# A decoder step with paged attention and a state-space branch: the issue order as a written list instead of a planner in the kernel

## The chip, the cores and the metric

The kernel runs on one core of a Trainium2 chip. The time is the device time of one execution in microseconds (us), here that of the only core. The core has five engines, each with an instruction queue of its own that is worked through in order: PE (matrix products), DVE (vector work), ACT (activations), POOL (a second vector engine, which also issues the gathers from the paged cache) and SP (which only issues transfers). ACT issues some small transfers as well. The trace is of one profiled execution.

## What is computed

One step of a trunk layer for a prompt of 512 tokens and, beside it, one new token for each of 8 running sequences with 4096 cached tokens. Everything is float32.

```python
def _pre(x, c, ...):                      # adaLN, RMSNorm, one input projection
    mod = silu(c) @ w_ada + b_ada
    shift, scale, gate = split(mod, 3)
    h = _rmsnorm(x, g_norm) * (1 + scale) + shift
    q, k, v, z_att, fl, u, z_ssm = split(h @ w_in, ...)
    logf = log_sigmoid(fl + b_fgate)
...
    o_att = _fox_prompt(q, k, v, logf)    # prompt: causal softmax(q k^T/8 + cum_i - cum_j) v
    y_ssm, h_re, h_im = _s5_scan(u, ...)  # complex diagonal recurrence
...
    k_past = cache_k[page_table]          # sample: 8 sequences x 4096 rows x 8 heads x 64
    v_past = cache_v[page_table]
    lf_past = cache_logf[page_table]
    o_att = _fox_sample(q, k, v, logf, k_past, v_past, lf_past)
...
def _post(...):
    att = o_att * silu(z_att)
    g = gelu(y_ssm)
    ssm = g * sigmoid(g @ w_glu + b_glu) * silu(z_ssm)
    return x + gate * (concat(att, ssm) @ w_out)
```

A final RMSNorm follows. The outputs are the two results, the new keys, values and log-forget gates, and the final states. The cached K and V that have to be read are 64 MB each, against some 20 MB of weights.

## The kernel before

The Python program records every engine call instead of issuing it. `Engine.__getattr__` hands each call to `Plan.add`, which makes a **step** of it; calls on PE that run side by side in the array (the four column strips of one product, for example) join the step before. There are 2881 steps, numbered in the order of recording: 1081 on PE, 712 on DVE, 792 on ACT, 235 on POOL, 61 on SP. `Plan.order()` then puts them in an order with a model of the chip: every step has a modelled cost, the steps that it depends on, and a key

```python
op.key = i - BEHIND * behind[i] + (TURN[i // GRP] if i // GRP < len(TURN) else 0)
```

where `i` is the step's number, `behind[i]` the modelled work that follows from it, and `TURN` a number for each group of 20 steps. Whenever an engine of the model comes free, it takes the ready step with the smallest key. On PE a ready step of the same tile shape is preferred if its key is less than `STAY = 150` higher. `issue()` (L427 to L429) emits the calls in that order, and each engine's queue on the chip holds its own steps in that order. All instructions therefore carry the line L429 and are told apart by engine, operation and tiles. Before an instruction an engine waits for whatever its operands need; the order of the queue is never changed on the chip.

The parts that the text speaks of:

- **The start.** SP loads `w_ada` in eight pieces of 1 MB (steps up to 20, L527), the prompt `x` in two halves (16 and 17, L523) and the first pieces of `w_in` (118 to 121). ACT squares the rows of x (86, 87), POOL makes the reciprocal roots (90 and 91, L597/598), ACT scales the four blocks of x by them (92 to 95, L651), PE transposes x (142 and following, L737). Beside that PE multiplies the conditioning vectors with the eight pieces of `w_ada` (96 to 103, L657), ACT copies the result out (104, L660), PE transposes it (105 to 108, L663), and DVE adds the bias (110, L670). DVE meanwhile builds the tables of the state-space branch. Step 527 (L1434) is the load of `d_skip` into the late part of arena A, on ACT's queue.
- **The cache.** Per sequence there are 8 K tiles and 8 V tiles of 128x2048 (1 MB each), 128 gathers in all, issued by POOL (`gather`, L634). A K tile is multiplied by the query, by POOL (128x1024 of it) and DVE (`dec_k`, L1307), and summed by ACT and DVE into the scores `sc`; `dec_soft` makes the softmax of a sequence; `dec_v` (L1345) multiplies a V tile with the weights on PE, eight matmuls of 128x32 into the tile `pv`. The tiles take five slots: three of the ring `kva` (tile `kv`) and two of arena A (`arA`); a gather waits until its slot has been used up.
- **The prompt.** Projections, state-space branch, attention and the output projection (L1594, six to ten pairs of 128x128 matmuls into `mm` at a time) share PE with the V products. Four small loads of `b_ada` (steps 1588 to 1591, L1467) go out on ACT's queue into arena B (`arB`), and the load of `w_glu` (1592, L1486) on SP's.
- **The tail.** After the last V tile come small matmuls for the sample rows (L1353, L1391, L1405), the samples' output projection and norm, and the stores.

The transfers of POOL, and those of SP and ACT, have their completion signals in rotation, eight for each of the two groups: a new issue of the same turn waits until the transfer eight before it has landed. The loads of ACT share the rotation with those of SP.

Of the kernel before, what the change touches and what calls it, by code (L numbers as in the profile page):

```python
# [13 lines left out]
BF16 = mybir.dt.bfloat16  # L14
# [22 lines left out]
TICK = 10240 / 3  # L37
BEHIND = 0.0005
STAY = 150
GRP = 20  # L40
XAT = 5
TURN = [
# [9 lines left out]
]  # L52
# [23 lines left out]
LAT = {"PE": (200, 5), "DVE": (190, 127), "ACT": (165, 200), "Pool": (90, 100), "SP": (90, 0)}  # L76
ACT_SET = {AF.Exp: 0, AF.Silu: 1, AF.Sin: 1, AF.Gelu_apprx_tanh: 2, AF.Sigmoid: 3, AF.Identity: 1}


class Op:  # L80
    __slots__ = ("eng", "calls", "cost", "dma", "deps", "tiles", "func", "tail", "load", "cols", "key", "mode", "lock",
                 "row", "desc")


class Engine:
    def __init__(self, plan, name, eng):
        self._p, self._n, self._e = plan, name, eng

    def __getattr__(self, method):
        return lambda *args, **kw: self._p.add(self._n, method, getattr(self._e, method), args, kw)  # L90


class Ring:


    def __init__(self, plan, pool, bufs, psum=False):
        self.p, self.pool, self.bufs, self.psum = plan, pool, bufs, psum

    def tile(self, shape, dtype, name, bufs=None):
        n = bufs or self.bufs  # L100
        t = self.pool.tile(shape, dtype, name=name, bufs=n)
        self.p.own(t, (id(self), name), n, self.psum)
        return t
# [25 lines left out]
class Plan:  # L129
    def __init__(self):  # L130
        self.ops, self.info, self.hist, self.rings = [], {}, {}, {}

    def own(self, t, ring=None, bufs=1, psum=False):
        a = t[:]
        w = int(np.prod(t.shape[1:]))
        self.info[a.tensor.name] = (w, ring, psum)
        if ring is not None:
            self.rings.setdefault(ring, (bufs, []))[1].append(a.tensor.name)

    def region(self, x):  # L140
        x = getattr(x, "ap", x) if isinstance(x, bass.IndirectOffsetOnAxis) else x
        if isinstance(x, (int, float, str, list, tuple, type(None))) or not hasattr(x, "to_broadcast"):
            return None
        a = x if hasattr(x, "offset") else x[:]
        i = self.info.get(a.tensor.name)
        if i is None:
            return None
        w = i[0]
        ap = [list(d) for d in a.ap]
        m = 1  # L150
        for step, n in ap[:0:-1]:
            if step:
                o = m
                if n > 1 and step > 0:
                    k = 1
                    while k < n:
                        j = min(k, n - k)
                        m |= m << (step * j) if j == k else m << (step * (n - k))
                        k += j
        size = int(np.prod([n for _, n in ap[1:]]))  # L160
        p0 = a.offset // w
        return a.tensor.name, p0, p0 + (ap[0][1] if ap[0][0] else 1), m << (a.offset % w), size, i[2]

    def add(self, eng, method, fn, args, kw):
        out = [args[0] if args else kw["out"], kw.get("accum_out")]
        outs = [r for r in map(self.region, out) if r]
        rest = list(args[1:]) + [v for k, v in kw.items() if k not in ("out", "accum_out")]
        ins = [r for r in map(self.region, rest) if r]
        cost = self.cost(eng, method, args, outs, ins, kw)
        deps, me = set(), len(self.ops)  # L170
        if cost is None:

            me -= 1
            op = self.ops[me]
            op.cost, op.tail = max(op.cost, self.product) + 27, 27
        else:
            op = Op()
            op.eng, op.calls, op.cost, op.deps, op.tiles, op.tail, op.load, op.cols = eng, [], cost, set(), set(), cost, 0, 0
            if eng == "PE":

                x = args[1]
                k, m = x.shape[0], int(np.prod(x.shape[1:]))
                op.load = m / 128 * (27 if x.dtype == BF16 else 107)
                op.mode = tuple(32 if d <= 32 else 64 if d <= 64 else 128 for d in (k, m))
            op.func = ACT_SET.get(args[2]) if method == "activation" else None

            op.lock = "dma" not in method and (eng == "Pool" or eng == "DVE" and (
                sum(not r[5] for r in ins) > 1 or method in ("tensor_copy", "tensor_scalar") and
                not any(r[5] for r in ins + outs)))
            r = (outs or ins)[0]  # L190
            op.dma, op.row, op.desc = self.transfer(args, kw, r) if "dma" in method else (0, 0, 0)
            self.ops.append(op)
        if eng == "PE":
            op.cols += self.columns
        for rw, rs in ((0, ins), (1, outs)):
            for name, p0, p1, m, size, psum in rs:
                h = self.hist.setdefault(name, ([], []))
                for lst in (h[0],) if rw == 0 else h:
                    deps.update(j for j, q0, q1, mm in lst if psum or (q0 < p1 and p0 < q1 and mm & m))
        for name, p0, p1, m, size, psum in outs:  # L200
            h = self.hist[name]
            for lst in h:
                lst[:] = [e for e in lst if not (psum or (p0 <= e[1] and e[2] <= p1 and not e[3] & ~m))]
            h[0].append((me, p0, p1, m))
        for name, p0, p1, m, size, psum in ins:
            self.hist[name][1].append((me, p0, p1, m))
        op.calls.append((fn, args, kw))
        op.deps |= deps - {me}
        op.tiles |= {r[0] for r in outs + ins if self.info[r[0]][1] is not None}

    def transfer(self, args, kw, r):

        total = r[4] * 4 * (r[2] - r[1])
        row = total
        for x in (args[0] if args else kw["out"], args[1] if len(args) > 1 else kw["in_"]):
            if "in_offset" in kw and x is kw["in_"]:
                continue
            a = x if hasattr(x, "offset") else x[:]
            n = 1
            own = a.tensor.name in self.info  # L220
            for step, m in [list(d) for d in a.ap][:0 if own else None:-1]:
                if m > 1 and step != n:
                    break
                n *= m
            row = min(row, n * 4)
        one = 8.5 + row / 25.5
        return max(total / row * one / 16, one), one, total / row / 16

    def cost(self, eng, method, args, outs, ins, kw):
        n = max([r[4] for r in outs + ins], default=1)  # L230
        ps = any(r[5] for r in outs + ins)
        if "dma" in method:
            return (1040 if "indirect" in method else 600) if eng == "Pool" else 480
        if eng == "PE":
            name, lo, hi, _, n, _ = outs[0]
            x = args[2] if method == "matmul" else args[1]
            passes = 2 if method == "transpose" else 1 if x.dtype == BF16 else 4
            self.columns = 0 if lo else n * passes * (ins[0][2] - ins[0][1]) / 128
            row, k = ins[0][1], ins[0][2] - ins[0][1]
            last, self.last_pe = self.last_pe, (name, lo, hi - lo <= 64, row, k <= 64 and method == "matmul")  # L240
# [1442 lines left out]
```

## Time and profile before

| | |
|---|---|
| median of 3 runs | 602.99 us |
| the runs | 595.1, 602.99, 1518.36 us |
| the profiled execution's own time | not listed; its span is 596.7 us |
| instructions | 9245 |
| granted TensorE clock, mean | 0.919 |
| transferred | 176.52 MB, mean 296 GB/s |
| by POOL's queue (q0) | 135.74 MB |
| by the queues of SP and ACT (q1) | 39.40 MB |

In the profile, "idle before" stands in brackets with the engine or transfer that ended it: `[5.51 <-ACT arA L429]` means that the engine stood for 5.51 us until ACT had written `arA`. A `q` behind an engine's name (ACTq) is the issue of a transfer by that engine's sequencer. `x24` behind a row is a number of equal instructions in a row. The chain of waits goes back from the last instruction to whatever released it. The rows of windows give the busy time of each engine in a stretch.

### The profile page before, as it was taken

How to read it: one execution, taken by the hardware profiler on the slowest of the kernel's cores; microseconds unless marked ns; L12 is line 12 of the kernel's file. 1: busy time of each engine (PE TensorE's matmuls, PEld its weight loads, DVE VectorE, ACT ScalarE, POOL GpSimd, SP SyncE). 2: the span in 40 equal slices, each digit the busy share in tenths (PEclk: the TensorE clock that was granted, in tenths of full speed). 3: DMA queues.
4: the chain of work that ended last, by engine and by line, in shares of the span. 5: the costliest groups of instructions: out<-in, count | busy, mean ns of one | idle time of the engine just before them, and what ended most of it. 6: DMA issues, size and time to landing. Idle time of an engine off the chain costs nothing.

```text
span 596.7 us, 9245 instructions
## 1 busy us (share of the span) xinstructions
PE 484.5 (81%) x3158; PEld 227.6 (38%) x3158; DVE 404.3 (68%) x712; ACT 289.2 (48%) x1354; POOL 323.5 (54%) x239
## 2 busy tenths in 40 slices
PE   3543669897888988299989899888589889999884
PEld 2111438743333435076633333333124334333222
DVE  6695899978999885237467957566655644664622
ACT  3043235435057454045463987678728865231301
POOL 6656109537217676255664785586637633864410
PEclk9855899997899999589999989999869989999988
DMA  7993545924409799868999899999979999997961
GB/s 226 391 371 130 163 138 182 362 77 141 142 24 350 267 395 403 344 228 303 393 365 399 302 403 359 359 397 396 389 284 334 356 411 397 370 322 287 372 263 39
DMA packets 45336, 176.52 MB, mean 296 GB/s; under 512 B 6980, under 2 KB 21736, under 8 KB 27880
## 3 DMA queue, kind: packets, MB, share of 16 engines
q0 software_dynamic: 19264, 135.74, 60.1%
q1 hardware_dynamic: 25376, 39.40, 18.8%
q10 hardware_dynamic: 648, 0.78, 0.4%
q8 instruction: 25, 0.41, 0.3%
q14 instruction: 23, 0.19, 0.1%
HBM read 171.48 MB, written 4.42 MB: 295 GB/s over the span
## 4 chain that ended last, share of the span: by engine, by line
PE 31%; DMA 24%; POOL 14%; DVE 13%; ACT 8%; issue 8%; SPq 2%; POOLq 0%; ACTq 0%; DVEq 0%
PE mm L429 22%; POOL kv L429 7%; POOL arA L429 6%; DMA arA<-in_cache_k_dram,kidx 6%; PE pv L429 6%; DMA w<-in_w_glu_dram 4%; DVE sc L429 4%; DVE arA L429 4%; DMA kv<-in_cache_v_dram,kidx 4%; DMA arA<-in_cache_v_dram,kidx 4%; DMA kv<-in_cache_k_dram,kidx 3%; DMA kv<-in_x_prompt_dram 3%; PE tr L429 2%; ACT arB L429 2%; SPq L429 2%
## 5 line engine op out<-in xcount | busy, mean ns | idle before, releaser
L429 PE MATMUL mm<-hT,w 128*128 128x512 f32 x256 | 135.9, 638 | 2.2 <-ACT qk L429 1.1
L429 POOL TENSOR_TENSOR kv<-kv,qs 128x1024 f32<-128x1024 f32 x38 | 90.1, 2373 | 30.9 <-DMA kv<-in_cache_k_dram,kidx 16.2
L429 ACT ACTIVATE kv<-kv 128x64 f32<-128x64 f32 x304 | 73.6, 245 | 55.2 <-DVE kv L429 37.9
L429 DVE TENSOR_REDUCE sc<-kv 128x24 f32<-128x1536 f32 x38 | 66.4, 1746 | 37.3 <-POOL kv L429 37.2
L429 ACT ACTIVATE arA<-arA 128x64 f32<-128x64 f32 (+2 forms) x215 | 52.3, 247 | 58.1 <-DVE arA L429 57.0
L429 POOL TENSOR_TENSOR arA<-arA,qs 128x1024 f32<-128x1024 f32 x26 | 61.8, 2376 | 17.5 <-DMA arA<-in_cache_k_dram,kidx 15.7
L429 POOL DMA_INDIRECT kv<-in_cache_v_dram,kidx x38 | 38.1, 1003 | 44.8 <-PE pv L429 10.8
L429 POOL DMA_INDIRECT kv<-in_cache_k_dram,kidx x38 | 37.4, 983 | 45.4 <-PE tr L429 16.8
L429 DVE TENSOR_REDUCE sc<-arA 128x24 f32<-128x1536 f32 x26 | 45.4, 1746 | 19.0 <-POOL arA L429 18.7
L429 PEld LDWEIGHTS mm<-hT,w 128*128 128x128 f32 x256 | 43.5, 200 | 37.8 <-issue 33.7
L429 ACT ACTIVATION_READ_ACCUMULATOR kv<-kv 128x1 f32 x304 | 57.7, 190 | 0.0
L429 DVE TENSOR_TENSOR kv<-kv,q 128x1024 f32<-128x1024 f32 x38 | 45.9, 1213 | 15.0 <-DMA kv<-in_cache_k_dram,kidx 13.7
L429 POOL DMA_INDIRECT arA<-in_cache_k_dram,kidx x26 | 25.6, 983 | 48.6 <-PE pv L429 24.0
L429 POOL DMA_INDIRECT arA<-in_cache_v_dram,kidx x26 | 25.4, 978 | 46.3 <-ACT arA L429 11.5
L429 PE MATMUL pv<-kv,arA 128*32 128x512 f32 x304 | 42.2, 632 | 9.6 <-DMA kv<-in_cache_v_dram,kidx 7.8
L429 DVE TENSOR_TENSOR arA<-arA,q 128x1024 f32<-128x1024 f32 x26 | 31.5, 1212 | 22.4 <-DMA arA<-in_cache_k_dram,kidx 22.4
L429 DVE TENSOR_TENSOR arA<-arA 128x512 f32<-128x512 f32 (+8 forms) x105 | 39.8, 406 | 1.3 <-ACT arA L429 1.0
L429 ACT ACTIVATION_READ_ACCUMULATOR arA<-arA 128x1 f32 x208 | 39.6, 190 | 0.0
L429 ACT ACT_TABLE_LOAD x26 | 33.4, 1283 | 8.5 <-DVE sc L429 5.0
L429 PE MATMUL pv<-arA 128*32 128x512 f32 x208 | 29.3, 636 | 6.7 <-DMA arA<-in_cache_v_dram,kidx 6.7
L429 PE MATMUL mm<-w,arB 128*128 128x512 f32 x64 | 33.7, 622 | 0.0
L429 PE MATMUL mm<-w,hT 128*128 128x256 f32 x128 | 33.4, 391 | 0.0
(245 smaller groups left out, 866.5 us busy)
## 6 DMA issues: line engine op xcount, KB each, us to landing
w<-in_w_in_dram SPq DMA_DIRECT2D x10, 1024.0 KB
w<-in_w_ada_dram SPq DMA_DIRECT2D x9, 1024.0 KB
qk<-in_w_ada_dram SPq DMA_DIRECT2D x2, 1024.0 KB
kv<-in_x_prompt_dram SPq DMA_DIRECT2D x2, 1024.0 KB
qk<-in_w_in_dram SPq DMA_DIRECT2D x2, 1024.0 KB
w<-in_w_out_dram SPq DMA_DIRECT2D x2, 1024.0 KB
qk<-in_w_out_dram SPq DMA_DIRECT2D x2, 1024.0 KB
hT<-in_x_prompt_dram SPq DMA_DIRECT2D x1, 2048.0 KB
```

The source lines that it names most:

```text
L429: fn(*args, **kw)
```

## The change

`Plan` with its costs, keys, `TURN`, `LAT` and the model is taken out. In its place stands a list `ORDER` of all 2881 step numbers, each once, and a class that issues the recorded steps in it. What `Plan.add` found out about joined PE calls is now said at the call by `join=`. The steps, their engines, their tiles, the rings and the arenas stay as they are.

```diff
-TURN = [
-    -13673, -11809, -11809, -9297, -10336, -3499, 59, -7594, -8009, -2496, -8525, -12911, -12961, -10094,
...
+ORDER = [
...
+]

 class Engine:
-    def __init__(self, plan, name, eng):
-        self._p, self._n, self._e = plan, name, eng
+    def __init__(self, steps, name, eng):
+        self._s, self._e = steps, eng

     def __getattr__(self, method):
-        return lambda *args, **kw: self._p.add(self._n, method, getattr(self._e, method), args, kw)
+        return lambda *args, join=False, **kw: self._s.add(getattr(self._e, method), args, kw, join)
...
+class Steps:
+    def __init__(self):
+        self.ops = []
+    def add(self, fn, args, kw, join):
+        if join:
+            self.ops[-1].append((fn, args, kw))
+        else:
+            self.ops.append([(fn, args, kw)])
+    def issue(self):
+        for i in ORDER:
+            for fn, args, kw in self.ops[i]:
+                fn(*args, **kw)
...
-class Plan:
...
-    def issue(self):
-        for i in self.order():
-            for fn, args, kw in self.ops[i].calls:
-                fn(*args, **kw)
...
-    plan = Plan()
+    plan = Steps()
...
             mm(t[32 * n:32 * n + 32], cs[:, k], wada[k][:, 512 * n:512 * n + 512],
-               start=(k == 0), stop=(k == 7))
+               start=(k == 0), stop=(k == 7), join=n > 0)
```

The list is not the one that `Plan.order()` gives. Compared engine by engine, a step's place differs for 1032 of PE's 1081 steps, 689 of DVE's 712, 753 of ACT's 792, 197 of POOL's 235 and 54 of SP's 61. By the longest common order, 589 steps of PE, 395 of DVE, 533 of ACT, 111 of POOL and 30 of SP have been moved past another one. Places of steps on their engine that the text uses, counted from 0:

| step | engine | what | place before | place in the list |
|---|---|---|---|---|
| 20 | SP | eighth load of `w_ada` | 17 | 13 |
| 96 | PE | first product with `w_ada` | 24 | 48 |
| 101 to 103 | PE | last products with `w_ada` | 63 to 73 | 59 to 61 |
| 142 | PE | first transpose of x | 65 | 86 |
| 90, 91 | POOL | reciprocal roots of x | 28, 29 | 17, 18 |
| 95 | ACT | scaling of the last block of x | 26 | 21 |
| 104 | ACT | copy of the adaLN row | 28 | 22 |
| 110 | DVE | adds the adaLN bias | 155 | 138 |
| 527 | ACT | load of `d_skip` | 11 | 113 |
| 1588, 1589 | ACT | loads of `b_ada` | 263, 272 | 330, 351 |
| 1590, 1591 | ACT | loads of `b_ada` | 273, 275 | 272, 296 |
| 1592 | SP | load of `w_glu` | 35 | 26 |
| 2750 | POOL | last V gather | 230 | 225 |
| 2776 | PE | product of the last V tile | 1065 | 1070 |
| 2838 to 2841 | PE | pairs of the output projection | 1067 to 1073 | 1044 to 1052 |

More of the change, by code (lines that the diff above doesn't have):

```diff
@@ L1 @@
-import heapq
 import math
-from collections import deque
 from contextlib import ExitStack
@@ L36 @@
 BK = 49.375
[L37 to L40, printed above, removed]
 XAT = 5
-TURN = [
[9 rows of a table removed]
-]
 SUF = 5
@@ L70, with __init__ @@
 NEG = -1e30
[L76 to L82, printed above, removed]
+ORDER = [
[151 rows of a table added]
+]
 class Engine:
-    def __init__(self, plan, name, eng):
-        self._p, self._n, self._e = plan, name, eng
+    def __init__(self, steps, name, eng):
+        self._s, self._e = steps, eng
     def __getattr__(self, method):
-        return lambda *args, **kw: self._p.add(self._n, method, getattr(self._e, method), args, kw)
+        return lambda *args, join=False, **kw: self._s.add(getattr(self._e, method), args, kw, join)
 class Ring:
-    def __init__(self, plan, pool, bufs, psum=False):
-        self.p, self.pool, self.bufs, self.psum = plan, pool, bufs, psum
+    def __init__(self, pool, bufs):
+        self.pool, self.bufs = pool, bufs
     def tile(self, shape, dtype, name, bufs=None):
[L100 to L103, printed above, removed]
+        return self.pool.tile(shape, dtype, name=name, bufs=bufs or self.bufs)
+class Steps:
[10 more added lines that the diff above has]
+                fn(*args, **kw)
 class Arena:
@@ L447, in ring @@
     def ring(name, bufs, **k):
-        return Ring(plan, ctx.enter_context(tc.tile_pool(name=name, bufs=bufs, **k)), bufs, "space" in k)
+        return Ring(ctx.enter_context(tc.tile_pool(name=name, bufs=bufs, **k)), bufs)
     cp, sm, wp, qkp, kva = (ring(n, b) for n, b in (("consts", 1), ("small", 2), ("w", 3), ("qk", 2), ("kva", 3)))
@@ L454, in tile_fox_s5_step @@
     arB = ar.tile([128, int(BK * 256)], F32, name="arB")
-    plan.own(arA)
-    plan.own(arB)
     sa = tb = Arena(arA)
@@ L701, in quarters @@
             for j in range(4):
-                mm(t[32 * j:32 * j + 32, 0:w], lhs(k), rhs(k, c0 + w * j, w), start=(k == 0), stop=(k == n - 1))
+                mm(t[32 * j:32 * j + 32, 0:w], lhs(k), rhs(k, c0 + w * j, w), start=(k == 0), stop=(k == n - 1),
+                   join=j > 0)
         return [(slice(c0 + w * j, c0 + w * j + w), t[32 * j:32 * j + 8, 0:w]) for j in range(4)]
@@ L951, in tile_fox_s5_step @@
                     mm(t[32 * j:32 * j + 32, 128 * q + 16 * a:128 * q + 128], Bzf[:, 32 * g + 16 * a:32 * g + 16 * a + 32],
-                       CA[:, g, 0:8 - a], start=(a == 0), stop=(a == 1), skip_group_check=True)
+                       CA[:, g, 0:8 - a], start=(a == 0), stop=(a == 1), skip_group_check=True, join=j > 0)
         ks.append(t.rearrange("p (q x) -> p q x", q=4))
@@ L977, in tile_fox_s5_step @@
         q = k % 4
-        mm(t[32 * q:32 * q + 32], wfl[:, k], hT[:, k], start=(k < 4), stop=(k >= 4))
+        mm(t[32 * q:32 * q + 32], wfl[:, k], hT[:, k], start=(k < 4), stop=(k >= 4), join=q > 0)
     e = sm.tile([128, 512], F32, name="e2")
@@ L1046, in ssm_phase @@
                         mm(t[64 * gh:64 * gh + 64, 256 * i:256 * i + 256], hT[:, k, tau:S:T],
-                           W["u", gh][:, k], start=(k == 0), stop=(k == 7))
+                           W["u", gh][:, k], start=(k == 0), stop=(k == 7), join=gh > 0)
             for i in range(2):
@@ L1085, in ssm_phase @@
                         mm(t[64 * gh:64 * gh + 64, 72 * j:72 * j + 72],
-                           BA[q][:, 4 * gh + j, 64 * i:64 * i + 64], U[:, 4 * q + j, gh])
+                           BA[q][:, 4 * gh + j, 64 * i:64 * i + 64], U[:, 4 * q + j, gh], join=gh > 0)
                 tv.append(t[:, 0:288].rearrange("p (j c) -> p j c", j=4))
@@ L1153, in ssm_phase @@
                     o = t[64 * gh:64 * gh + 64, 128 * j:128 * j + 128]
-                    mm(o, U[:, 4 * q + j, gh, 0:NCH], Toep[:, gh, j, 128 * q:128 * q + 128], start=True, stop=False)
+                    mm(o, U[:, 4 * q + j, gh, 0:NCH], Toep[:, gh, j, 128 * q:128 * q + 128], start=True, stop=False, join=gh > 0)
                     mm(o, Hst[:, g, 0:NCH], CA[:, g, 1:], start=False, stop=True)
@@ L1255, in attn @@
                     r = slice(64 * hh, 64 * hh + 64)
-                    mm(t[hh][:, 0:n], qT[r, m, d], kT[r, m, 0:n], start=False, stop=True)
+                    mm(t[hh][:, 0:n], qT[r, m, d], kT[r, m, 0:n], start=False, stop=True, join=hh > 0)
                 nm = sm.tile([128, 2], F32, name="nm")
@@ L1277, in attn @@
                     mm(o[64 * hh:64 * hh + 64, 128 * kb:], vn[:, kb, 128 * m + 64 * hh:128 * m + 64 * hh + 64],
-                       PT[hh][:, kb, 128 * kb:], start=(kb == 0), stop=(kb == 3), skip_group_check=True)
+                       PT[hh][:, kb, 128 * kb:], start=(kb == 0), stop=(kb == 3), skip_group_check=True, join=hh > 0)
             acopy(attT[:, m], o)
@@ L1345, in dec_v @@
             mm(pv[32 * r:32 * r + 32], pzs[b % 2][:, 4 * c + r], vt[:, 512 * r:512 * r + 512],
-               start=(b % 4 == 0 and c == 0), stop=(b % 4 == 3 and c == 7))
+               start=(b % 4 == 0 and c == 0), stop=(b % 4 == 3 and c == 7), join=r > 0)
         if b % 4 == 3 and c == 7:
@@ L1405, in samp_out @@
                 mm(t[32 * j:32 * j + 32, 0:256], mTs[:, k0 + k],
-                   res["wo"][2 * (j // 2) + k0 // 4][:, k, 256 * (j % 2):256 * (j % 2) + 256], start=(k == 0), stop=(k == 3))
+                   res["wo"][2 * (j // 2) + k0 // 4][:, k, 256 * (j % 2):256 * (j % 2) + 256], start=(k == 0), stop=(k == 3),
+                   join=j > 0)
         o = sm.tile([128, 256], F32, name="e2")
@@ L1480, in gate_part @@
                     mm(gt[32 * j:32 * j + 32, 0:256], cs[:, 2 * i + k], gw[i][:, k, 256 * j:256 * j + 256],
-                       start=(k == 0), stop=(k == 1))
+                       start=(k == 0), stop=(k == 1), join=j > 0)
             V.tensor_add(gsb, gsb, gt[:, 0:256])
```

274 lines of the change are left out of this document (removed), and 159 rows, old and new, of tables (ORDER, TURN).

## The prediction

> **What bounds the kernel now.** I read the page first for the engines and the chain, then windows of 25 us for the stages, then the waits inside those stages.
>
> ```profile
> span 596.7 us, 9245 instructions
> PE 484.5 (81%) x3158; PEld 227.6 (38%) x3158; DVE 404.3 (68%) x712; ACT 289.2 (48%) x1354; POOL 323.5 (54%) x239
> PE 31%; DMA 24%; POOL 14%; DVE 13%; ACT 8%; issue 8%; SPq 2%; POOLq 0%; ACTq 0%; DVEq 0%
> ```
>
> No engine is busy throughout and the chain passes through all of them: the limit changes from stage to stage. The profiled execution's own time is not listed; its span of 596.7 lies 6.3 under the median of 602.99 (the 1518.36 is an outlier) and 1.6 over the run of 595.1. Those two runs differ by 1.3%, so about 2% is what a measurement here tells from no change.
>
> ```profile
> 25.00:50.00 25.00, 7.92 (x35) 2.98 (x35) 20.04 (x41) 8.40 (x15) 14.34 (x2) 0.51 0.94 334
> 75.00:100.00 25.00, 20.26 (x242) 14.89 (x236) 24.35 (x44) 12.77 (x74) 11.42 (x6) 0.93 0.37 128
> 175.00:200.00 25.00, 22.94 (x97) 8.95 (x94) 24.75 (x41) 17.06 (x81) 17.22 (x12) 1.00 0.84 298
> 250.00:275.00 25.00, 21.60 (x149) 15.81 (x149) 11.09 (x17) 10.70 (x69) 12.58 (x9) 0.85 0.65 230
> 375.00:400.00 25.00, 21.36 (x190) 8.93 (x190) 16.10 (x20) 17.00 (x85) 17.03 (x13) 1.00 0.99 377
> 525.00:550.00 25.00, 25.00 (x78) 9.64 (x74) 12.63 (x13) 6.37 (x36) 15.21 (x14) 1.00 0.84 305
> ```
>
> The columns after the window are busy us of PE, weight loads, DVE, ACT and POOL, then granted clock, DMA share and GB/s. Up to about 200 us **DVE** is the limit (24.35 and 24.75 of 25) and the DMA is half empty. From 275 us the **gathers** are (0.99 at 377 GB/s), and from 500 us **PE** shares the limit with them (25.00). The row of 250 to 275 is neither: 230 GB/s, no engine full.
>
> **The change, part by part.** The steps, their engines and their tiles stay; what moves is each engine's queue order. I compared the two orders engine by engine, taking durations from this trace. Nearly every step has another place (1032 of 1081 on PE, 197 of 235 on POOL), but a near one: the mean shift is 11 places on PE, 15 on DVE, 12 on ACT, 2.8 on POOL, 2.7 on SP. So the stages and their limits should stay, and only particular waits change. Building the list happens before the device runs and costs nothing there.
>
> (1) The start. The rows below are of ACT, DVE and POOL.
>
> ```profile
> 28.38 0.28 ACTq L429 DMA_DIRECT2D arA<-in_d_skip_dram  x1
> 28.71 1.19 ACT L429 ACTIVATE arA<-sm 64x512 f32<-64x512 f32 x2 [14.95 <-DMA kv<-in_x_prompt_dram]
> 29.93 0.69 DVE L429 TENSOR_TENSOR arB<-arA 128x512 f32<-128x512 f32 x1 [5.51 <-ACT arA L429]
> 36.56 16.20 POOL L429 TENSOR_SCALAR arA<-arA 128x4 f32<-128x4 f32 x1 [10.66 <-ACT hT L429]
> 52.85 1.05 POOL L429 TENSOR_TENSOR arA<-arA,nhalf 128x4 f32<-128x4 f32 x1
> 61.77 0.37 DVE L429 TENSOR_TENSOR arA<-tr,arA 128x72 f32<-128x72 f32 x2 [9.06 <-PE tr L429]
> 89.35 3.48 DVE L429 TENSOR_TENSOR kv<-kv,q 128x1024 f32<-128x1024 f32 x3 [0.19 <-ACT qs L429]
> 18.36 12.79 SPq L429 DMA_DIRECT2D w<-in_w_ada_dram  x2
> ```
>
> Before 89 us DVE has two large gaps. The first, 5.51 us, waits for ACT copies that stand behind ACT's own issue of the d_skip load (step 527), which was held until a half of x_prompt had landed. The list puts 527 from ACT place 11 to 113, near 100 us of the old clock, so this wait goes. The second, 9.06 us, waits for the transposed adaLN row (step 110). That needs ACT's copy 104, which now stands ahead of three of the four x scalings instead of behind all, and PE's steps 101 to 108, which now stand ahead of the x transposes. But one scaling (step 95) is still ahead of 104, and it needs POOL's steps 90 and 91, the 16.20-us row. That row did not end until DVE stopped. In the list DVE reaches step 110 after about 46 us of work (place 138, before 155), so about half of the gap can stay. Against this, SP's eighth w_ada load (step 20; the second of the 12.79-us row) has been drawn ahead of three other loads and still waits for PE step 96, now behind 36 transposes (place 48, before 24); I estimate a hole in the loads of 3 to 4 us, bounded by nothing and the 12.79 us of that row. Sum: −5.5 −4 to −5 + 4 = about **−5 us**; bounds −14.6 (both gaps gone) and +4. DVE, the limit up to 200 us, carries a lead on to the gathers.
>
> (2) The hole at 250 us.
>
> ```profile
> 243.24 0.79 ACTq L429 DMA_DIRECT2D arB<-in_b_ada_dram  x2
> 244.08 0.60 ACT L429 ACTIVATE arB<-tr 128x512 f32<-128x512 f32 x1 [6.21 <-DMA w<-in_w_in_dram]
> 252.39 0.32 ACTq L429 DMA_DIRECT2D arB<-in_b_ada_dram  x1
> 252.75 0.60 ACT L429 ACTIVATE arB<-tr 128x512 f32<-128x512 f32 x1 [8.07 <-DMA w<-in_w_glu_dram]
> 255.54 0.98 POOL L429 DMA_INDIRECT arA<-in_cache_v_dram,kidx  x1 [11.45 <-ACT arA L429]
> ```
>
> ACT twice stands at the issue of a small b_ada load until a 1-MB SP load has landed, 14.28 us in all; the copies behind it wait, then PE, then POOL's next gather (11.45 us). The window of 250 to 275 moved 230 GB/s where 375 to 400 moved 377: (377−230)·25 us = 3.7 MB, 9.7 us at 377. The list moves two of the four b_ada loads (1588 and 1589) from places 263 and 272 to 330 and 351, 1591 from 275 to 296, leaves 1590 at 272, and puts the w_glu load nine SP places earlier. One at a time they can be held again, where copies stand behind them just the same. Bounds: −9.7, and 0 if the four, held one at a time, stop ACT for as long in all. I take a value near the middle: **−4 us**.
>
> (3) PE's tile shapes.
>
> ```profile
> 412.35 0.86 PE mm L429 x2
> 498.29 2.71 PE pv L429 x24
> 525.34 19.08 PE mm L429 x44
> 546.47 0.99 PE pv L429 x8
> 547.47 1.05 PE mm L429 x2
> 548.52 1.00 PE pv L429 x8
> ```
>
> In the chain, a pair of matmuls of 128x128 among its like takes 0.86 us, and a V product (eight of 128x32) 2.71/3 = 0.90. Where they alternate, the pair takes 1.05 and the product 1.00: 0.29 us for two changes of shape, 0.145 each, or 0.10 if only the product's side is counted. The old order has 353 changes, the list 245; after 475 us 75 and 30. Those 45 cost 4.5 to 6.5 us where PE is full: **−5 us**. The other 63 lie where DVE or the gathers are the limit and count as nothing; without that cover they would be 6 to 9 more.
>
> (4) The tail.
>
> ```profile
> 573.47 0.94 POOL L429 DMA_INDIRECT arA<-in_cache_v_dram,kidx  x1 [1.89 <-PE pv L429]
> 579.06 1.06 PE L429 MATMUL pv<-arA 128*32 128x512 f32 x8
> 584.56 1.10 PE L429 MATMUL mm<-qk,arB 128*128 128x512 f32 x2
> 591.89 0.48 DVE q_s L429
> ```
>
> The last V tile is issued at 573.47 and multiplied at 579.06. Behind it the old order still has 7.8 us of PE work, with output-projection pairs between the small matmuls of the sample rows; the list leaves 3.7, by doing four of those five pairs earlier. 4.1 us at most, nothing if the pairs only push the V product back; PE was full just before, so I take **−1.5 us**.
>
> (5) V tiles held. Five slots take all the gathered tiles, and a gather is issued when its slot is free.
>
> ```profile
> 515.63 0.94 POOL L429 DMA_INDIRECT kv<-in_cache_v_dram,kidx  x1 [0.68 <-DVE e L429]
> 516.60 2.37 POOL L429 TENSOR_TENSOR arA<-arA,qs 128x1024 f32<-128x1024 f32 x1
> kv<-in_cache_v_dram,kidx POOLq DMA_INDIRECT x35, 8.6
> ```
>
> The tile issued at 515.63 lands some 8.6 us later and is used in the product at 546.47, behind the 19.08 us of projection: 22 us lost to one slot of five. Eleven of the 59 V tiles after 195 us wait over 11 us. I summed PE's work ahead of each product in both orders: of eight of them the product comes 6.5 to 13.6 us earlier, together 79 slot-us, 16 us over five slots if each refills at once. Against it POOL's order puts one more multiply (2.37 us) ahead of most V gathers, and four gathers come 10 to 21 us of POOL work later, together 60 slot-us, 12 us. The difference is **−3 us**; bounds −16 and +12, both kept for the range.
>
> Sum: −5 −4 −5 −1.5 −3 = −18.5. From the profiled 596.7 that is 578, from the median 584.5; I state **583**, close to the median because that is the base of the comparison.
>
> **The rivals.**
>
> *Given back* (no change). Parts 1 and 2 bring gathers forward to a time when the DMA is at 0.99, and they queue there; part 5 cancels. Then parts 3 and 4 alone are left: 603 − 6.5 = 596. For it: the DMA share in 375 to 400. Against it: the DMA is at 0.37 and 0.65 in two quoted windows, so bytes do fit earlier.
>
> *POOL's queue turns* (slower). A multiply at the head of POOL waits for its K tile, or for DVE, with a V gather behind it whose slot is free. One multiply of 2.37 us for each of 59 V gathers is 140 slot-us, 28 us over five slots; with the four late gathers 40, less the 16 freed: +24, and +12 if half the multiplies have their K tile ready. With the leads of 1 and 2 lost in the same queue: 615 to 627, say 620. It decides once the added lateness of the V gathers passes the 79 slot-us that PE frees. For it: POOL is in order and has 14% of the chain. Against: K gathers are issued 1 to 10 us of POOL work earlier, so the multiply's tile should be there.
>
> *The start keeps its length.* POOL's two 128x4 rows took 16.20 and 1.05 us; the first ran beside a DVE without a gap, the second as DVE stood. If the second DVE gap only grows by what the first loses, part 1 is nothing: 603 − 13.5 = 589.5. [...]
>
> *All of it pays*: −9 −9.7 −6.5 −4 −8 = −37, 566. It needs the gathers to run at 400 GB/s, while the best quoted window shows 377.
>
> That the list is only the planner's order written down is excluded by the places above.
>
> **The numbers.** Forecast (574 to 592) 0.41; given back 0.21; POOL's queue 0.14; start keeps its length 0.10; all of it 0.14. Faster by over 2% (under 591) is the forecast, all of it, and half of the start case: 0.60. Slower by over 2% (over 615) 0.13, within 2% 0.27. Range **564 to 612**: it takes in every case but the slow one and the far end of the large one.
>
> **What would show it.** Part 1: no 5.51-us gap of DVE near 25 us, and the first K multiply on DVE at 78 to 86 us instead of 89.35. Part 2: the windows from 225 to 300 all over 340 GB/s, ACT's waits behind b_ada below 5 us. Part 3: PE's busy time down by about 10 us in all, from 484.5. Part 4: under 14 us from the last V product to the end (before 17.6). Part 5: the long V waits in the list gone, POOL's idle time before gathers down. I am wrong if POOL or DVE shows new waits for K gathers of over 15 us in all, if the w_ada load holds SP's queue past 30 us, or if the b_ada loads stop ACT again.

## The result and the profile after

The new kernel takes **578.32 us** (median of 4 runs, 576.52 to 581.5) against 602.07 for the old one beside it. The ratio is **0.966, with a 95% interval of 0.958 to 0.974**; in a second comparison it was 0.967 (0.962 to 0.972). The forecast was 583. Ratios here leave disturbed executions out and medians do not, so a ratio can differ a little from the quotient of two medians; three of the traces below (the b_ada loads alone, the eight moved DVE steps, the reverse on the new list) are of disturbed executions, and mainly their local rows are used.

The profiled execution spans 574.5 us, 22.2 less than before. The head, the engines, the chain and the rows of POOL's gathers on the page of the new kernel:

```profile
span 574.5 us, 9192 instructions
PE 471.2 (82%) x3158; PEld 227.6 (40%) x3158; DVE 405.3 (71%) x712; ACT 288.4 (50%) x1353; POOL 315.4 (55%) x239
DMA 35%; DVE 18%; PE 13%; issue 11%; POOL 8%; ACT 5%; POOLq 0%; DVEq 0%; ACTq 0%
L245 POOL DMA_INDIRECT kv<-in_cache_k_dram,kidx x38 | 37.6, 988 | 58.7 <-PE pv L245 13.3
L245 POOL DMA_INDIRECT kv<-in_cache_v_dram,kidx x38 | 37.7, 992 | 42.3 <-PE pv L245 20.2
L245 POOL DMA_INDIRECT arA<-in_cache_k_dram,kidx x26 | 25.2, 969 | 37.4 <-PE pv L245 25.5
L245 POOL DMA_INDIRECT arA<-in_cache_v_dram,kidx x26 | 25.3, 975 | 18.6 <-ACT arA L245 7.6
```

The chain now runs over transfers (35%, before 24%) and much less over PE (13%, before 31%). POOL's idle time ahead of its gathers adds up to 157.0 us. The windows of the new kernel, same columns as before:

```profile
25.00:50.00 25.00, 12.23 (x73) 5.41 (x73) 24.86 (x54) 10.62 (x15) 13.93 (x11) 0.80 0.86 308
175.00:200.00 25.00, 23.77 (x103) 9.14 (x96) 20.31 (x24) 17.46 (x71) 20.27 (x14) 1.00 0.90 325
250.00:275.00 25.00, 23.28 (x181) 15.09 (x174) 13.10 (x19) 12.09 (x65) 15.58 (x11) 1.00 0.97 366
300.00:325.00 25.00, 20.82 (x76) 8.28 (x75) 14.40 (x23) 17.16 (x79) 13.55 (x10) 0.86 0.82 298
525.00:550.00 25.00, 22.69 (x91) 8.16 (x89) 10.57 (x20) 4.26 (x25) 11.06 (x11) 1.00 0.93 368
```

DVE is full from 25 to 50 us (24.86, before 20.04). The hole at 250 is gone (366 GB/s, before 230). But 300 to 325 moves 298 GB/s, where the old kernel moved 386:

```profile
300.00:325.00 25.00, 21.45 (x143) 8.56 (x141) 17.42 (x25) 10.18 (x47) 14.73 (x11) 1.00 1.00 386
```

The clearest view of where the time went compares the same step in two traces. The table gives by how many us a V product starts earlier (minus) than in the old kernel's trace:

| V product (step) | old start | new | start alone | start + b_ada | three edits | rest alone |
|---|---|---|---|---|---|---|
| 1st (1004) | 174.2 | −18.8 | −22.0 | −21.3 | −13.8 | +1.6 |
| 13th (1337) | 262.5 | −23.3 | −11.2 | −23.8 | −25.2 | −3.5 |
| 21st (1612) | 313.2 | −28.2 | −11.1 | −23.1 | −23.6 | −10.8 |
| 25th (1737) | 342.3 | −15.9 | −10.8 | −23.7 | −23.2 | +1.8 |
| 45th (2387) | 477.6 | −12.4 | −11.4 | −22.9 | −23.3 | +4.7 |
| 64th (2776) | 579.1 | −18.3 | −11.3 | −24.3 | −25.9 | +0.2 |
| end | 596.7 | −22.2 | −11.6 | −24.5 | −26.2 | −4.1 |

The column "new" shows that the prediction's sum came out right by parts that were not: 19 us are won before the first V product and 28 by 313 us, 12 are given back by 342 and 3.5 more by 478, then 6 are won up to the last product and 4 behind it. A second trace of the same new kernel has −18.6, −20.9, −26.6, −15.3, −9.6, −13.5 and −17.6 in these rows: the same shape, but up to 5 us apart. A difference of that size between two columns tells nothing by itself. The other columns are the experiments below.

### The profile page after: what moved, and what is told of

It reads as the page before. It is cut to its first block, busy times and chain, and to the rows that moved or that the text cites. A ratio compares the mean times of both kernels' runs of the same rounds, so it can differ in the third digit from the quotient of the medians.

```text
span 574.5 us, 9192 instructions
## 1 busy us (share of the span) xinstructions
PE 471.2 (82%) x3158; PEld 227.6 (40%) x3158; DVE 405.3 (71%) x712; ACT 288.4 (50%) x1353; POOL 315.4 (55%) x239
## 4 chain that ended last, share of the span: by engine, by line
DMA 35%; DVE 18%; PE 13%; issue 11%; POOL 8%; ACT 5%; POOLq 0%; DVEq 0%; ACTq 0%
DMA kv<-in_cache_k_dram,kidx 16%; PE mm L245 9%; DMA kv<-in_cache_v_dram,kidx 7%; DVE arA L245 6%; DMA arA<-in_cache_v_dram,kidx 6%; POOL kv L245 5%; DVE sc L245 5%; DMA arA<-in_cache_k_dram,kidx 4%; PE pv L245 3%; DVE kv L245 3%; POOL arA L245 3%; ACT arB L245 2%; DVE arB L245 2%; ACT kv L245 1%; DVE hT L245 1%
## 5 line engine op out<-in xcount | busy, mean ns | idle before, releaser
L245 PE MATMUL mm<-hT,w 128*128 128x512 f32 x256 | 130.1, 631 | 1.3 <-PE pv L245 0.6
L245 ACT ACTIVATE arA<-arA 128x64 f32<-128x64 f32 (+1 forms) x215 | 52.4, 246 | 50.4 <-DVE arA L245 47.9
L245 POOL DMA_INDIRECT kv<-in_cache_k_dram,kidx x38 | 37.6, 988 | 58.7 <-PE pv L245 13.3
L245 PEld LDWEIGHTS mm<-hT,w 128*128 128x128 f32 x256 | 45.7, 198 | 47.6 <-issue 42.9
L245 DVE TENSOR_TENSOR arA<-arA 128x512 f32<-128x512 f32 (+9 forms) x105 | 45.2, 452 | 0.8
L245 POOL DMA_INDIRECT arA<-in_cache_k_dram,kidx x26 | 25.2, 969 | 37.4 <-PE pv L245 25.5
L245 PE MATMUL mm<-qk,hT 128*64 128x256 f32 x256 | 32.9, 419 | 7.2 <-ACT arA L245 7.0
L245 PE MATMUL pv<-arA 128*32 128x512 f32 x208 | 28.5, 623 | 11.2 <-DMA arA<-in_cache_v_dram,kidx 8.3
L245 POOL DMA_INDIRECT arA<-in_cache_v_dram,kidx x26 | 25.3, 975 | 18.6 <-ACT arA L245 7.6
L245 PEld LDWEIGHTS mm<-qk,hT 128*64 128x64 f32 x256 | 26.1, 201 | 12.9 <-ACT arA L245 7.4
```

What stands on the lines that cost most here:

```text
L245: fn(*args, **kw)
```

## The experiments

### Splitting the list at 180 us

The list is cut at the steps that started before 180 us in the old trace.

```diff
 start alone:  ORDER = [new list's order, steps before 180 us] + [old order, the others]
 rest alone:   ORDER = [old order, steps before 180 us] + [new list's order, the others]
```

> The steps that started before 180 us in the old trace are issued in the new list's order, all later ones in the old order. Theory 'the start carries it': the K and V gathers around 200 us run about 19 us earlier than in the old kernel and the lead is kept, with the hole near 250 us still there: 582 to 588 us. Rival 'given back': the gathers of the middle are bound by the transfers and the lead is used up: 595 to 603 us.

> The reverse: old order up to 180 us, new list's order behind it. Theory 'the start carries it': only the hole (7 us), the giving back (minus 10) and the tail (4 us) are left, so 598 to 603 us. Rival 'the V products and the shapes on PE pay': 588 to 594 us.

Measured: start alone 587.71 us, ratio 0.981 (0.970 to 0.993); rest alone 597.99, ratio **1.000** (0.994 to 1.005). The order of everything behind 180 us, put on the old start, is as a whole worth nothing that can be measured, and the rival (588 to 594 us) falls. That is a sum and not an absence: in its trace a lead of 10.8 us at the 21st product is lost by the 25th, and 9 us are won behind the 45th. But the start alone does not bring the whole gain either: its lead of 22 us at the first V product is 11 at the 13th. Its hole is still there. A piece of its chain (start, us, what), and the ACT row where that piece ends:

```profile
214.05 26.76 DMA w<-in_w_glu_dram
```

```profile
241.20 0.60 ACT L239 ACTIVATE arB<-tr 128x512 f32<-128x512 f32 x1 [9.66 <-DMA w<-in_w_glu_dram]
```

The chain spends 26.76 us on one load of w_glu, because a b_ada issue on ACT stands until that load has landed, and behind it stands a copy that PE's next transposes need (56 matmuls in the chain).

### The hole: the b_ada loads alone, and with the new start

```diff
 ACT's queue, places of 1588, 1589, 1590, 1591:
-263, 272, 273, 275
+345, 346, 347, 348    (behind step 1510, about 300 us)
```

> Old order; only the four b_ada loads stand some 75 to 85 places later on ACT (near 300 us). Theory 'ACT's held issues make the hole at 250 us and it costs the end': no ACT wait behind b_ada, the windows of 240 to 260 us over 340 GB/s, V products at 260 to 300 us 6 to 9 us earlier, and 594 to 597 us. Rival 'given back': the hole is gone but the later gathers are not earlier, 599 to 604 us.

> New list's order up to 180 us, old order behind it, and the four b_ada loads later on ACT as in the kernel with this edit alone. Theory 'start and hole add up': the run with the new start alone gave a ratio of 0.981 and lost 27 us of its chain to the w_glu load behind which b_ada stood; without it 576 to 581 us, all of the new kernel's gain. Rival 'the two leads use the same transfers': 584 to 588 us.

Alone: 595.9 us, ratio **0.990** (0.984 to 0.995). With the new start: 580.49 us, 0.978 (0.967 to 0.990), profiled span 572.1. The window of the hole, alone and then with the new start:

```profile
250.00:275.00 25.00, 22.96 (x124) 15.38 (x125) 16.83 (x24) 11.32 (x69) 16.85 (x13) 0.93 0.96 359
```

```profile
250.00:275.00 25.00, 25.00 (x139) 16.53 (x132) 13.46 (x15) 11.84 (x77) 15.60 (x13) 1.00 0.96 373
```

In both it moves 359 to 373 GB/s, before 230. With the new start the 13th V product is 12.6 us earlier than without the edit (−23.8 against −11.2) and the lead is still there at the end. The two ratios (0.981 and 0.978) have intervals that overlap, so the ratios do not tell the two apart. The times do: all four runs with the edit (573.82 to 583.79 us) lie under all four of the start alone (584.63 to 593.79), though on another chip; the traced run is the fastest of its four. Of the single edit's 10.5 us at the 13th product, 2.3 are left at the end of its trace.

The list itself removes the hole by other means. It issues the w_glu load 37 us earlier, of which its lead at that time explains some 20, and spreads the four b_ada loads:

```profile
226.44 0.40 SPq L429 DMA_DIRECT2D w<-in_w_glu_dram  x1
189.52 0.37 SPq L245 DMA_DIRECT2D w<-in_w_glu_dram  x1
```

In its trace no ACT row from 218 to 285 us waits for a transfer.

### The start: the d_skip load alone

```diff
 ACT's queue, place of 527:
-11
+113
```

> Old order; only the d_skip load (step 527) stands later on ACT, near the place that the list gives it. Theory as predicted: the 5.51-us gap of DVE goes, POOL's row ends 5 us earlier because DVE stops earlier, time 596 to 599 us. Rival 'another wait takes its place': DVE's gap only moves, 601 to 605 us.

595.04 us, ratio **0.991** (0.985 to 0.997). The time lies 1 us under the expected range; the gap and the end of POOL's row came as expected. POOL's row and DVE's remaining gap in its trace:

```profile
33.73 13.40 POOL L239 TENSOR_SCALAR arA<-arA 128x4 f32<-128x4 f32 x1 [7.91 <-ACT hT L239]
56.57 0.37 DVE L239 TENSOR_TENSOR arA<-tr,arA 128x72 f32<-128x72 f32 x2 [9.51 <-PE tr L239]
```

The 5.51-us gap is gone. POOL's row still lasts until DVE stops at 47 us, and the second gap is as long as it was (9.51).

### The start: eight neighbouring DVE steps

In the old order, DVE's last product that reads PSUM (step 281, `arA<-mm,arA`) ends at 36.45 us, just before POOL's row becomes ready at 36.56, and only products with two operands in SBUF follow, for 16 us. Eight neighbours change places; the product that reads PSUM comes 1.2 us later, and three short products (395 to 397, 128x128) come earlier, to just ahead of it:

```diff
 DVE's queue:
-281, 398, 282, 395, 399, 396, 400, 397
+398, 395, 396, 397, 281, 282, 399, 400
```

> Old order; eight neighbouring steps of DVE change places so that one product that reads PSUM (arA<-mm,arA) runs about 1 us later, just when POOL's 128x4 row is ready, inside what was a run of products with both operands in SBUF. Theory 'POOL is shut out by DVE's run of two-SBUF-operand products': POOL's row falls from 16.20 us to under 3 us, DVE's 9.06-us gap to under 2 us, time 592 to 596 us. Rival 'POOL is busy with the gathers ahead of it': row and time unchanged, 600 to 605 us.

592.53 us, ratio **0.988** (0.977 to 0.998). POOL's rows and DVE's products in its trace:

```profile
36.41 0.36 POOL L239 TENSOR_SCALAR arA<-arA 128x4 f32<-128x4 f32 x1 [10.52 <-ACT hT L239]
36.85 1.09 POOL L239 TENSOR_TENSOR arA<-arA,nhalf 128x4 f32<-128x4 f32 x1
45.79 8.35 POOL L239 DMA_INDIRECT kv<-in_cache_k_dram,kidx  x1 [7.85 <-PE mm L239]
36.43 0.28 DVE L239 TENSOR_TENSOR arA<-arA 128x128 f32<-128x128 f32 x1
36.74 0.29 DVE L239 TENSOR_TENSOR arB<-arB,arA 128x128 f32<-128x128 f32 x1
36.95 0.68 DVE L239 TENSOR_TENSOR arA<-mm,arA 128x512 f32<-128x512 f32 x1
```

POOL's row falls from **16.20 to 0.36 us**, the second row starts just ahead of the PSUM product, and DVE's 9.06-us gap does not occur. POOL's queue ahead of the row is the same as before, so the rival falls: what DVE runs at that moment sets the length of POOL's row, 16.20 or 0.36 us. Which of the moved steps let POOL in, this run does not show, since by the profile's times, which are rough for POOL, the first row ends at 36.77, among the short products and ahead of the PSUM one. That DVE's products there have two operands in SBUF does not decide it alone: so have the run, mostly of 128x512, beside which the row took 16.20 us, and the short products beside which it took 0.36.

The new list does the same by another hand: it strews short steps and copies out of PSUM into DVE's run. Its POOL and DVE rows, in order of time:

```profile
34.59 0.20 POOL L245 TENSOR_SCALAR arA<-arA 128x4 f32<-128x4 f32 x1 [11.48 <-ACT hT L245]
34.60 0.21 DVE L245 COPY arB<-arA 64x16 f32<-64x16 f32 x1
34.87 2.04 POOL L245 TENSOR_TENSOR arA<-arA,nhalf 128x4 f32<-128x4 f32 x1
36.76 0.15 DVE L245 COPY gcol<-tr 128x12 f32<-128x12 f32 x1
37.10 3.31 POOL L245 DMA_INDIRECT suf<-in_cache_logf_dram,lidx  x1 [0.18 <-issue]
40.19 0.41 DVE L245 COPY arA<-sm 128x256 f32<-128x256 f32 x1
```

POOL gets through about where such a step stands: its row of 2.04 us ends by the copy out of `tr` at 36.76, the gather issue of 3.31 us by the copy out of `sm` at 40.19.

I also tried the reverse on the new list:

```diff
 DVE's queue of the new list:
+331, 52, 46, 74, 53 ahead of 303       (from places 116 to 132 to place 109)
+391 behind 110                         (from place 131)
```

> The new list with six small steps of DVE moved: five stand about 5 us earlier, the one that copies from PSUM (arA<-sm) behind the addition of the adaLN bias, so that DVE's run of products with two SBUF operands has no gap between the moment when POOL's 128x4 rows are ready (34.6 us) and that addition. Theory 'POOL is shut out by such a run': one of POOL's two rows takes 6 us or more, a DVE gap of 7 to 10 us appears near 43 us, and the time rises to 583 to 588 us. Rival 'the new place of POOL's gathers is what helped': row, gap and time as in the new kernel, 575 to 581 us.

579.49 us, ratio 0.975 (0.964 to 0.985), against 0.966 and 0.967 for the list itself: inconclusive, and the expectation was missed.

```profile
34.37 1.27 POOL L239 TENSOR_SCALAR arA<-arA 128x4 f32<-128x4 f32 x1 [12.00 <-ACT hT L239]
35.72 4.02 POOL L239 TENSOR_TENSOR arA<-arA,nhalf 128x4 f32<-128x4 f32 x1
43.52 0.23 DVE L239 TENSOR_TENSOR arA<-tr,arA 128x72 f32<-128x72 f32 x1 [1.42 <-PE tr L239]
```

Both rows became longer (1.27 and 4.02 us), the gap is only 1.42, and the lead at the first V product is 20.8 us, no smaller than the list's own. By the profile POOL's rows ended at 35.6 and at 39.7 although every step of DVE there has two SBUF operands; short ones (128x16) stand near the first of these moments, and only 128x512 ones at the second. What lets POOL through there is not settled.

### The three edits together

All three on the old order, with the PSUM product further back because DVE now runs 5.5 us ahead. PE, POOL and SP keep the old order in every place.

```diff
 ACT: 527 to place 113; 1588 to 1591 behind 1510
 DVE, behind 398:
+395, 396, 397, 406, 319, 304, 310, 281, 282, 399, 400
```

> Old order with three local edits and nothing else: the d_skip load late on ACT, one PSUM-reading product of DVE moved to where POOL's 128x4 rows are ready (later in DVE's order than in the run with that edit alone, since DVE runs 5.5 us ahead), the four b_ada loads late on ACT. PE, POOL and SP keep the old order. Theory 'three held waits are the gain': the ratios of the single edits, 0.9875, 0.991 and 0.990, make 0.969, so 578 to 584 us against 598. Rival 'the new order of PE, POOL and SP is needed to keep the leads': 588 to 594 us.

**573.83 us, ratio 0.961 (0.955 to 0.967)**; the new kernel beside it 576.81. This is faster than the 578 to 584 expected from the single ratios. The traces show where: with the d_skip or the b_ada edit alone 7 to 8 us of lead are lost between the 21st and the 25th V product, with the three together nothing. Why is not known.

> The new kernel unchanged, on the same chip as the two above, so that they are compared with it directly: 574 to 582 us by every theory.

The head of its page, and POOL's rows:

```profile
span 570.5 us, 9245 instructions
PE 474.3 (83%) x3158; PEld 223.1 (39%) x3158; DVE 403.9 (71%) x712; ACT 288.9 (51%) x1354; POOL 308.0 (54%) x239
```

```profile
33.90 0.20 POOL L239 TENSOR_SCALAR arA<-arA 128x4 f32<-128x4 f32 x1 [8.25 <-ACT hT L239]
34.18 1.05 POOL L239 TENSOR_TENSOR arA<-arA,nhalf 128x4 f32<-128x4 f32 x1
33.69 0.68 DVE L239 TENSOR_TENSOR arA<-mm,arA 128x512 f32<-128x512 f32 x1
```

Here the first row lies wholly within the product that reads PSUM. Three held waits, undone by moving five issues and eleven DVE steps, are worth as much as the whole list. The list's start wins 22.0 us at the first V product, the three edits 13.8; no run shows where the other 8 come from, and at the 13th they are gone.

### Is there something better than both?

The old middle on the new start and end, three combinations:

```diff
 m_320_500:  new list to 320 us, old order to 500, new list behind
 best500:    new list to 180 us, old order to 500 with b_ada late, new list behind
 three_500:  the three edits to 500 us, new list behind
```

> New list's order for the steps that started before 320 us in the old trace and for those from 500 us on, old order between. The new kernel led by 28 us at 313 us and by 13 us at 394. Theory 'the middle of the new list gives the lead back': the lead of some 25 us is kept and the tail adds 4 to 8: 568 to 574 us, faster than both. Rival 'the transfers set the middle whatever the order': the lead falls to 12 to 15 us there as well, 576 to 582 us.

582.99 us, 0.981 (0.968 to 0.994): the lead fell from 26 us at the 21st V product to 12 at the 25th, as the rival said. Its reason does not hold, though: with the old order from 180 us on and the b_ada loads late, the lead stays (−23.1 and −23.7). The list's order up to 320 us is enough to lose it.

> New list's order up to 180 us and from 500 us on, old order between, b_ada late on ACT. Theory 'start, hole and tail add': the run without the tail had a ratio of 0.978 and a profiled span of 572; the tail's 4 us make 568 to 575 us, faster than the new kernel. Rival 'the end is set by the transfers of the last V tiles': 576 to 582 us, as the new kernel.

572.89 us, 0.960 (0.954 to 0.966), profiled span 564.3.

> The old order with the three local edits (ratio 0.961), and from 500 us on the new list's order. Theory 'the new tail is worth its 4 us by itself': from the last V product to the end under 14.5 us instead of 17.6, and a ratio of 0.952 to 0.956, 569 to 571 us against 598. Rival 'the pairs done earlier only push the last V products back': tail shorter, last V product later, ratio 0.959 to 0.964.

571.11 us, 0.960 (0.954 to 0.966), profiled span 566.2. From the last V product to the end it has 13.3 us, the three edits alone 17.3: the tail is shorter by 4.0 in the trace, as expected, but the ratio (0.960 against 0.961) lies in the rival's range. From the 45th V product to the last it takes 100.7 us, the three edits 98.8: part of the gain seems to be paid there, by the pairs done earlier. This run and the one before it have the lowest medians of the study, 4 to 6 us under the new kernel beside or near them; their intervals overlap with the new kernel's (0.962 to 0.972).

### Where the new list gives the lead back

Between the 21st and the 25th V product the lead falls by 12.3 us with the list, by 12.6 with the rest alone and by 13.9 with the list to 320 us; with the old middle behind the new start it falls by nothing. So the list's order at this place, or just ahead of it, gives back. But the place is a weak one in the old order too: the traces with the b_ada and the d_skip edit alone lose 7.3 and 7.7 us there. PE and POOL rows of the list, and a window:

```profile
312.18 1.93 PE L245 MATMUL pv<-kv,arA 128*32 128x512 f32 x8 [3.87 <-DMA kv<-in_cache_v_dram,kidx]
314.31 1.91 PE L245 MATMUL mm<-hT,w 128*128 128x512 f32 x2
314.42 0.97 POOL L245 DMA_INDIRECT kv<-in_cache_v_dram,kidx  x1 [4.57 <-PE pv L245]
319.04 0.94 POOL L245 DMA_INDIRECT arA<-in_cache_k_dram,kidx  x1 [3.65 <-PE pv L245]
```

```profile
314.00:318.00 4.00, 4.00 (x14) 1.55 (x14) 0.00 (x0) 1.51 (x5) 0.97 (x1) 0.60 0.48 133
```

A V product stands at the head of PE before its tile is there. PE waits 3.87 us, the granted clock is then 0.60, the product and the pair of matmuls take 1.93 and 1.91 instead of about 1 us, two gathers wait for the slots, and the transfers fall to 133 GB/s. The second trace of the new kernel and the rest alone show the same wait (3.98 and 3.69 us). It is not the whole of the loss: with the list to 320 us PE waits at most 0.44 us for a V tile at this place, and 13.9 us are lost all the same. No run here changed only these steps, so the cause stays open.

## Why the prediction was right, and where it was not

**The time** (583 predicted, 578.3 measured) and the direction held, by a sum whose terms were mis-sized both ways.

**Part 1, the start: −5 predicted, 16.0 us of lead at the first K product on DVE, and 11.6 left at the end when the start stands alone.** The failed step is "about half of the gap can stay". I read from the 16.20-us row that POOL gets through only when DVE stops, and looked for where DVE would stop. What counted in the runs is what DVE ran when POOL was ready: within a product out of PSUM the row took 0.20 us (three edits), among three short products 0.36 (eight moved steps), and the list, where it took 0.20, has a short copy right there. So both gaps went, and the lead passed even the bound of −14.6; the DVE gaps left before 60 us are

```profile
15.19 0.23 DVE L245 COPY arA<-tr 128x64 f32<-128x64 f32 x1 [1.51 <-PE tr L245]
57.09 3.94 DVE L245 TENSOR_REDUCE arA<-suf 128x64 f32<-128x2048 f32 x1 [1.41 <-issue]
```

and four of 0.7 to 0.9 us before 8 us. The first K product on DVE came at 73.35 us, earlier than the 78 to 86 I had given as a sign. The late w_ada load was no cost that shows, so the +4 has no run behind it: 46 transposes stand ahead of step 96 in the list, not 36, yet the load went out at 22.26 us, where the old row of 12.79 us ended at 31.15. The reading "up to about 200 us DVE is the limit and the DMA is half empty" was too wide: DVE had 15.94 us in the window of 50 to 75 and 18.04 in that of 125 to 150, and the DMA share was 0.94 from 25 to 50. The rival "the start keeps its length" did not happen: the second gap did not grow by what the first lost, and POOL's row took 0.20 us although DVE is busy for 24.86 of the 25 us from 25 to 50.

**Part 2, the hole: −4 predicted, −6 alone by its ratio (0.990) and 12.6 us at the 13th product on the new start.** The wait "one at a time they can be held again" did not occur. This is the term that I took near the middle of its bounds and that came out at the far one, or beyond it.

**Part 3, the shapes: −5 predicted; 4 us less of PE's busy time shown behind the 45th V product; what it is worth in time is not shown by itself.** The sign I had named, PE's busy time down by about 10 us, came true (484.5 to 471.2). Over the whole kernel it proves nothing: with the three edits PE is busy for 474.3 us, in the old order of PE, with every change of shape in it; the granted clock is 0.955 there and was 0.919. The stretch from the 45th to the last V product tells more. It holds the same V products and nearly the same pairs (134 and 136 matmuls), with 67 changes of shape in the old order of PE and 23 in the list. At one granted clock, the three edits first and the rest alone second:

```profile
454.30:553.20 98.90, 94.44 (x391) 33.43 (x392) 49.96 (x68) 34.62 (x174) 49.85 (x40) 0.98 0.94 361
482.30:579.30 97.00, 90.31 (x395) 36.61 (x394) 51.59 (x71) 33.56 (x181) 47.02 (x40) 0.98 0.91 355
```

PE is busy for 4.1 us less with 44 changes fewer, 0.09 us for one, near the 0.10 of the prediction's working. The stretch lasts 98.8 to 101.8 us in the seven traces with the old order there and 95.5 to 99.2 in the four with the list's. That the changes of shape alone do this is argued, since all of the order differs there; and the two traces of the new kernel differ by 2 us in this stretch.

**Part 4, the tail: −1.5 predicted; −4 behind the last V product, about −2 in all.** It lasts 17.3 to 18.1 us in the seven traces without the new end and 13.3 to 13.7 in the seven with it. For the new kernel:

```profile
559.86 1.90 PE L245 MATMUL pv<-arA 128*32 128x512 f32 x16
569.69 0.48 DVE q_s L245
```

The first row holds the last two products, the second of them from 560.7; the last row ends the chain. But the pairs done earlier cost part of it ahead of the last V product. From the 45th product to the end, the list's order from 500 us on makes 114.0 us of the three edits' 116.2, and 115.4 of the 117.4 of the new start with late b_ada loads. That is near the −1.5.

**Part 5, V tiles: −3 predicted, 12 us lost between 313 and 342 us.** POOL's idle time before gathers did fall (185.1 to 157.0), but a slot that is free earlier needs a tile's use that is not late. In three traces the earlier product put PE behind a tile that was still under way, for 3.7 to 4.0 us; I had counted PE's work ahead of the products and not the landing of the tiles. That this explains all 12 is not shown. The rival "POOL's queue turns" did not happen; "given back" did, but only for a part.

One sign that I had given for being wrong came true: new waits of POOL or DVE for K gathers of over 15 us in all. DVE's rows, before and after:

```profile
L429 DVE TENSOR_TENSOR kv<-kv,q 128x1024 f32<-128x1024 f32 x38 | 45.9, 1213 | 15.0 <-DMA kv<-in_cache_k_dram,kidx 13.7
L429 DVE TENSOR_TENSOR arA<-arA,q 128x1024 f32<-128x1024 f32 x26 | 31.5, 1212 | 22.4 <-DMA arA<-in_cache_k_dram,kidx 22.4
L245 DVE TENSOR_TENSOR kv<-kv,q 128x1024 f32<-128x1024 f32 x38 | 46.0, 1213 | 35.0 <-DMA kv<-in_cache_k_dram,kidx 28.1
L245 DVE TENSOR_TENSOR arA<-arA,q 128x1024 f32<-128x1024 f32 x26 | 31.5, 1213 | 34.9 <-DMA arA<-in_cache_k_dram,kidx 31.3
```

DVE waits 23 us more for K gathers and POOL 20 us more, and the kernel is faster all the same, with more of its chain on transfers. The sign was badly chosen: an engine that has its other work done earlier waits longer for the same transfers.

## What to carry to other kernels

Compare two traces of the same steps as a lead over time, and cut the change in time before asking what it does: of some 1660 steps moved past another, three held waits carry as much as the whole list. Look for waits where a cheap instruction is held by something that it does not need: a small transfer's issue behind a large load (6.21 and 8.07 us on ACT here), or a short POOL row beside a gapless DVE run (16.20 us); each was undone by moving a few steps. A sign that comes true, such as PE's busy time, supports a step only if a run without that step does not show it, so look for a stretch with the same work at the same granted clock. And trace the same kernel twice before reading a few us of lead.

## What the runs showed of the hardware

The order of eight DVE steps alone changed a POOL row of 128x4 from 16.20 to 0.36 us; in the run with the three edits the row took 0.20 us within a DVE product that reads PSUM. The issue of a gather took longer as well: in the trace of the eight moved steps the first K gather took 8.35 us beside a run of two-operand products, where 0.94 to 1.06 is usual, but in that of the three edits it took 1.26 beside such a run. And a V product took 1.93 us and the pair of matmuls behind it 1.91, after PE had waited 3.87 us for the tile and with a granted clock of 0.60 in the window behind the wait, where about 1 us is usual for each: some 1.8 us on top of the wait itself.
